# Attention value matmuls gathered behind a step's last key tile, and the softmax sums turned by transposes

## The chip, the core and the metric

The kernel runs on one core of a Trainium2 chip. The metric is the device time of one execution in microseconds (us); the time before is the median of three runs.

## What is computed

Two transformer blocks over 1024 latent positions and 256 context positions, model width 1024. The first has two layers, each with a grouped-query attention beside a convolution, a gated recurrence and a Fourier mix; the second has one latent attention of 16 heads beside a state-space scan, then a feed-forward part. The change touches only the two attentions:

```python
def attend(qb, k, v):                       # first block: 4 query heads, 2 key/value heads, width 64
    s = jnp.einsum("bhgqd,bhkd->bhgqk", qb, k).astype(jnp.float32) * (HEAD_DIM ** -0.5)
    p = jax.nn.softmax(s, axis=-1).astype(v.dtype)
    return jnp.einsum("bhgqk,bhkd->bhgqd", p, v)

def attend_2(q_nope, q_rope, k_nope, k_rope, v):      # second block: 16 heads, value width 64
    s = (jnp.einsum("bqhd,bkhd->bhqk", q_nope, k_nope)
         + jnp.einsum("bqhr,bkr->bhqk", q_rope, k_rope)) * ATTN_SCALE
    p = jax.nn.softmax(s.astype(jnp.float32), axis=-1).astype(v.dtype)
    return jnp.einsum("bhqk,bkhd->bqhd", p, v)
```

Keys are the 1024 latent positions and the 256 of the context: 1280, or ten tiles of 128. The first block's first layer also lets the 256 context queries attend to the two context tiles.

## The kernel before

Both attentions work in **steps**: one head and one block of queries (512, or the 256 of the context). The first block (GQA) has 8 full steps and 4 context steps in its first layer and 8 full steps in its second; the second block's latent attention (MLA) has 32 full steps. That makes 48 full steps of ten key tiles and 4 steps of two.

A step has two parts, and the second part of a step runs beside the first part of the next one. `put_max` finds the largest score of each query, roughly: TensorE multiplies queries by keys (L600 in GQA, L1350 in MLA, twelve matmuls a step), VectorE reduces each result (L459) and all of them (L462), TensorE turns the result into a row (L465), and ScalarE writes that row beside the queries (L466), so that the score matmuls subtract it. `weigh` then loops over the key tiles: scores on TensorE (L613 and L614 in GQA, L1360 to L1362 in MLA) into one of three PSUM tiles `t`, the exponential on ScalarE into a tile `e` (L501), and the running sum of the `e` tiles: two of three on GpSimd (`ea`, L492 then L495), the third on VectorE (`eb`). L519 adds `eb` to `ea` at the end.

The **value matmuls** (L480) multiply a tile of values (128 keys by 64 columns, the stationary operand) with a tile `e` (128 by 512, moving), all in float32. The two matmuls of a pair write the two halves of `o`: the even key tile partitions 0 to 63, the odd one 64 to 127, and each half is summed up by itself. A pair is sent while the loop runs, as soon as one later tile (GQA) or two (MLA) wait behind it:

```python
            waiting.append((v(j), e))
            self.dense(wait)
            if len(waiting) >= lag + 2:
                values([waiting.pop(0), waiting.pop(0)])
```

`weigh_end` finishes a step: four matmuls of `ea` with a column of ones give the 512 sums as four columns (L533), VectorE takes the reciprocal (L535), four transposes spread it (L538), ScalarE copies the upper half of `o` (L540), VectorE adds the halves (L541) and scales them (L542), and the result is stored. It is called inside the next step, behind key tile `tail` (the first number of `GQA_STEPS` and `MLA_STEPS`), so its matmuls stand among the next step's scores. `self.small` is the PSUM tag for its small tiles: `t` in GQA, `mm` (three tiles as well, shared with L1350) in MLA.

The rows of an engine are not in the order of the code: a scheduler that builds the program moves an instruction ahead of others where its operands let it. `dense(us)` asks for that much work of another part of the program (projections, L344 and L213) to be laid between.

Of the kernel before, what the change touches and what calls it, by code (L numbers as in the profile page):

```python
# [16 lines left out]
ALU = mybir.AluOpType  # L17
AX = mybir.AxisListType
# [3 lines left out]
P = 128  # L22
# [55 lines left out]

GQA_STEPS = 4, 4, 1, 0.5
MLA_STEPS = 3, 5, 2, 0.4

FOURIER_WAIT = 1.0
HGRN_WAIT = 12.0, 1.0, 3.0, 2.0, 2.0, 3.0
# [4 lines left out]
class Kern:  # L90
# [377 lines left out]
    def weigh(self, pool, out, keys, n, scores, v, beside, pieces, steps):  # L468

        V, G, S, PE = self.V, self.G, self.S, self.PE
        tail, ahead, lag, wait = steps
        o = self.psum("o")[:, :n]
        waiting, sent = [], []

        def values(pair):
            for h, (vj, e) in enumerate(pair):
                PE.matmul(o[64 * h:64 * h + 64], vj, e, start=not sent, stop=len(sent) == len(keys) // 2 - 1)  # L480
            sent.append(1)


        sums = {}

        def count(i, e):
            E = V if i % 3 == 2 else G
            if E not in sums:
                sums[E] = [e]
            elif len(sums[E]) == 1:  # L490
                total = self.ctmp(pool, "ea" if E is G else "eb", (P, 512), 2)[:, :n]
                E.tensor_tensor(total, sums[E][0], e, op=ALU.add)  # L492
                sums[E] = [total, total]
            else:
                E.tensor_tensor(sums[E][0], sums[E][0], e, op=ALU.add)  # L495

        done = 0
        for i, j in enumerate(keys):
            s = scores(j)
            e = self.ctmp(pool, "e", (P, 512), 6)[:, :n]  # L500
            S.activation(e, s, AF.Exp)  # L501
            count(i, e)
            waiting.append((v(j), e))
            self.dense(wait)
            if len(waiting) >= lag + 2:
                values([waiting.pop(0), waiting.pop(0)])
            if i == tail:
                self.weigh_end()
            while beside and done < pieces and done * (len(keys) - ahead) < (i + 1) * pieces:
                done += 1  # L510
                next(beside, None)
        for _ in beside or ():
            pass
        self.weigh_end()
        while waiting:
            values([waiting.pop(0), waiting.pop(0)])
        total = sums[G][0]
        if V in sums:
            G.tensor_tensor(total, total, sums[V][0], op=ALU.add)  # L519
        self.pending = pool, out, o, total  # L520

    def weigh_end(self):
        if not self.pending:
            return
        pool, out, o, total = self.pending
        self.pending = None
        V, S, PE = self.V, self.S, self.PE

        n = o.shape[1]
        nq = n // P  # L530
        t = self.psum(self.small)
        for a in range(nq):
            PE.matmul(t[:, a:a + 1], total[:, a * P:(a + 1) * P], self.one)  # L533
        r = self.tmp("sl", (P, 4), bufs=3)[:, :nq]
        V.reciprocal(r, t[:, :nq])  # L535
        b = self.psum(self.small)[:, :n]
        for a in range(nq):
            PE.transpose(b[:, a * P:(a + 1) * P], r[:, a:a + 1].to_broadcast([P, P]), self.ident)  # L538
        u = self.tmp("nt")[0:64, :n]
        S.activation(u, o[64:128], AF.Copy)  # L540
        V.tensor_tensor(u, o[0:64], u, op=ALU.add)  # L541
        V.tensor_tensor(u, u, b[0:64], op=ALU.mult)  # L542
        self.store(out, u)
# [42 lines left out]
    def gqa(self, pool, layer, src, need_ctx, y):  # L586
# [22 lines left out]
        def weigh(i, t0, m, h, b, beside, pieces):  # L609
            def scores(j):  # L610
# [7 lines left out]
            self.weigh(pool, y[2 + i][64 * h:64 * h + 64, t0:t0 + m], keys, m, scores,  # L618
                       lambda j: vt[:, j, i], beside, pieces, GQA_STEPS)


        for i in range(2):
            ks[i] = self.gqa_keys(pool, kd, i)
            qs[i] = self.gqa_queries(pool, src[f"q{i}"], layer, n)
            self.dense(4.0)
            last = None
            for t0, m in ALL if n == TA else LAT:
                for h in range(2):
                    b, piece, pieces = maxima(i, t0, m, h)
                    if last:  # L630
                        weigh(*last, piece, pieces)
                    else:
                        for _ in piece:
                            pass
                    last = i, t0, m, h, b
            weigh(*last, None, 0)
# [669 lines left out]
    def mla(self, pool, more, kv, done, beside, y):  # L1306
# [48 lines left out]
        def weigh(p, h, t0, m, beside):  # L1355
            def scores(j):
# [9 lines left out]
            self.weigh(pool, y[p][64 * h:64 * h + 64, t0:t0 + m], range(nk), m, scores, lambda j: v[:, j, a], beside, 12,  # L1366
                       MLA_STEPS)

# [6 lines left out]
        for p in range(8):  # L1375
            for h in range(2):
                for t0, m in LAT:

                    now = maxima(p, h, t0, m)
                    if last:  # L1380
                        weigh(*last, now)
                    else:
                        for _ in now:
                            self.dense(MLA_WAIT[2])
                        self.dense(MLA_WAIT[3])
                    last = p, h, t0, m
                    if p in (1, 7):
                        next(beside, None)
                    if t0 == 0 and p + h == 0:
                        operands(0, 1)  # L1390
                    elif t0 == 0:

                        nxt = 2 * p + h + 1
                        if nxt < 16:
                            operands(nxt // 2, nxt % 2)
                        if nxt in (4, 6, 10):
                            vt[len(vt)] = values(len(vt))
# [659 lines left out]
```

## Time and profile before

| | |
|---|---|
| time, median of 3 runs | 4227.44 us (4225.31 to 4230.69) |
| the profiled execution | 4237.05 us, of it a span of 4234.8 us |
| TensorE busy | 3954.1 us, 93% of the span |
| VectorE, ScalarE, GpSimd busy | 2392.5, 1685.9 and 1518.5 us (56%, 40%, 36%) |
| value matmuls (L480), busy | 238.5 us in MLA, 142.8 us in GQA |
| matmuls of the sums (L533), busy | 32.3 us in MLA, 18.8 us in GQA |
| mean granted TensorE clock | 0.96 of full speed |

Busy time of TensorE is modelled from starts, and neighbouring matmuls overlap in it: what one costs is read from the distance between starts. A float32 matmul leaves two records, two passes, so that a pair of value matmuls is "x4" in a row, a single one "x2". PEld is the loading of the stationary operand.

### The profile page before, as it was taken

The numbers are of one execution on the slowest core, as the hardware profiler recorded it, in microseconds if no ns is written. First come the engines' busy times: TensorE is split into PE (matmuls) and PEld (weight loads), VectorE is DVE, ScalarE is ACT, GpSimd is POOL, SyncE is SP. The second block draws the span as 40 slices with busy tenths as digits, with TensorE's granted clock in tenths as the row PEclk, the third lists the DMA queues.
The fourth block names the chain that finished last, engine by engine and source line by source line (L and its number), as shares of the span: only waits on it lengthen the run. The fifth ranks groups of instructions, "written<-read, shape, count | busy, mean of one in ns | idle before, by whom it ended". The sixth has DMA issues, their size and how long they took to land.

```text
span 4234.8 us, 55709 instructions
## 1 busy us (share of the span) xinstructions
PE 3954.1 (93%) x19762; PEld 2918.6 (69%) x19762; DVE 2392.5 (56%) x4158; ACT 1685.9 (40%) x3047; POOL 1518.5 (36%) x1336
## 2 busy tenths in 40 slices
PE   6999999999999988988999979999999989999998
PEld 3765577667775567666677665655555979988987
DVE  6355487855455487678778774554445365324331
ACT  5333444345334544354343343333334334333332
POOL 3223301126314321154122233455455444445443
PEclk8999999999999989998999999999999989999999
DMA  5541122256541221254534566422212364333232
GB/s 175 165 127 60 53 82 91 85 170 208 170 154 58 63 72 59 88 189 128 164 123 159 184 204 186 127 76 60 48 41 80 120 208 127 95 114 121 93 112 86
DMA packets 273914, 500.26 MB, mean 118 GB/s; under 512 B 30978, under 2 KB 76578, under 8 KB 270628
## 3 DMA queue, kind: packets, MB, share of 16 engines
q1 hardware_dynamic: 269636, 467.75, 35.2%
q0 software_dynamic: 4000, 28.97, 2.9%
q8 instruction: 155, 2.54, 0.3%
q14 instruction: 123, 1.01, 0.1%
HBM read 377.39 MB, written 119.21 MB: 117 GB/s over the span
## 4 chain that ended last, share of the span: by engine, by line
PE 43%; DVE 7%; DMA 3%; issue 2%; ACT 1%; POOL 1%; SPq 0%; DVEq 0%; ACTq 0%; POOLq 0%
PE mm L213 21%; PE o L480 5%; PE mm L344 4%; PE t L1360 2%; PE mm L1350 2%; DVE sp L1165 2%; PE t L1361 2%; PE t L1362 2%; PE t L1589 1%; PE o L1567 1%; PE mm L533 1%; PE t L1524 1%; DMA xt<-xtok 0%; ACT sw L1557 0%; POOL wl L204 0%
## 5 line engine op out<-in xcount | busy, mean ns | idle before, releaser
L204 POOL TENSOR_TENSOR wl<-wr,wh 128x512 fp32r<-128x512 f32 (+2 forms) x641 | 861.0, 1350 | 1555.7 <-ACT wh L203 1346.2
L203 ACT ACTIVATE wh<-wr 128x512 fp32r<-128x512 f32 (+1 forms) x822 | 502.5, 620 | 793.7 <-PE mm L213 246.5
L344 PE MATMUL mm<-xh,wh 128*128 128x512 f32 (+1 forms) x1704 | 667.0, 392 | 11.8 <-DVE sp L169 2.9
L344 PE MATMUL mm<-xh,wl 128*128 128x512 f32 (+1 forms) x1704 | 652.0, 383 | 5.4 <-POOL wl L204 5.3
L344 PE MATMUL mm<-xl,wh 128*128 128x512 f32 (+1 forms) x1704 | 652.9, 384 | 1.8 <-POOL xl L324 1.2
L501 ACT ACTIVATE e<-t 128x512 f32<-128x512 f32 (+1 forms) x488 | 287.4, 594 | 504.7 <-PE t L1362 320.5
L495 POOL TENSOR_TENSOR ea<-ea,e 128x512 f32<-128x512 f32 x240 | 307.3, 1280 | 377.9 <-ACT e L501 365.9
L344 PEld LDWEIGHTS mm<-xh,wh 128*128 128x128 f32 x1704 | 332.1, 195 | 86.3 <-issue 9.5
L344 PEld LDWEIGHTS mm<-xh,wl 128*128 128x128 f32 x1704 | 331.9, 195 | 74.7 <-POOL wl L204 9.5
L344 PEld LDWEIGHTS mm<-xl,wh 128*128 128x128 f32 x1704 | 333.2, 196 | 66.9 <-issue 7.6
L213 PE MATMUL mm<-fxh,wh 128*128 128x512 f32 (+2 forms) x1056 | 339.6, 323 | 2.9 <-ACT fxh L1741 2.1
L213 PE MATMUL mm<-fxh,wl 128*128 128x512 f32 (+2 forms) x1056 | 341.3, 323 | 0.0
L213 PE MATMUL mm<-fxl,wh 128*128 128x512 f32 (+2 forms) x1056 | 340.6, 323 | 0.4 <-DVE fxl L1742 0.3
L459 DVE TENSOR_REDUCE sm<-mm 128x1 f32<-128x512 f32 (+1 forms) x384 | 209.8, 590 | 52.3 <-PE mm L1350 52.1
L480 PE MATMUL o<-e,v 128*64 128x512 f32 x640 | 238.5, 618 | 0.0
L213 PEld LDWEIGHTS mm<-fxh,wh 128*128 128x128 f32 x1056 | 201.4, 191 | 19.0 <-ACT fxh L1741 2.6
L213 PEld LDWEIGHTS mm<-fxl,wh 128*128 128x128 f32 x1056 | 201.9, 191 | 17.4 <-DVE fxl L1742 1.7
L213 PEld LDWEIGHTS mm<-fxh,wl 128*128 128x128 f32 x1056 | 201.9, 191 | 15.5
L204 DVE TENSOR_TENSOR wl<-wr,wh 128x512 fp32r<-128x512 f32 x181 | 134.9, 757 | 72.5 <-ACT wh L203 64.3
L459 DVE TENSOR_REDUCE sm<-t 128x1 f32<-128x512 f32 (+1 forms) x200 | 112.7, 590 | 80.0 <-PE t L600 78.8
L1779 DVE TENSOR_SCALAR fc<-gs,vecs 128x512 f32<-128x512 f32 x44 | 54.5, 1238 | 165.3 <-ACT gs L1775 165.2
L480 PE MATMUL o<-e,vt 128*64 128x512 f32 (+1 forms) x336 | 142.8, 608 | 0.0
(469 smaller groups left out, 8032.9 us busy)
## 6 DMA issues: line engine op xcount, KB each, us to landing
wr<-w_mod SPq DMA_DIRECT2D x192, 256.0 KB, 3.0
wr<-w_in SPq DMA_DIRECT2D x190, 256.0 KB, 3.0
wr<-w_up SPq DMA_DIRECT2D x176, 256.0 KB, 2.6
wr<-w_out SPq DMA_DIRECT2D x144, 256.0 KB, 3.1
wr<-w_down SPq DMA_DIRECT2D x80, 256.0 KB, 2.7
q<-qd POOLq DMA_DIRECT2D x16, 768.0 KB, 6.7
rope<-rope SPq DMA_DIRECT2D x20, 512.0 KB, 4.4
k<-kd POOLq DMA_DIRECT2D x16, 640.0 KB, 7.8
```

The lines of the kernel that those rows point to most:

```text
L203: self.S.activation(hi, raw, AF.Copy)
L204: (next(subs) if subs else self.G).tensor_tensor(lo, raw, f32(hi), op=ALU.subtract)
L213: self.PE.matmul(out, a, b, start=i == 0, stop=i == n - 1)
L344: self.PE.matmul(ps, a, b, start=at + i == 0, stop=at == k_tiles - 1 and i == 2)
L459: V.tensor_reduce(m[:, a, c:c + 1], scores(a, c), axis=AX.X, op=ALU.max, negate=True)
L480: PE.matmul(o[64 * h:64 * h + 64], vj, e, start=not sent, stop=len(sent) == len(keys) // 2 - 1)
L495: E.tensor_tensor(sums[E][0], sums[E][0], e, op=ALU.add)
L501: S.activation(e, s, AF.Exp)
L1165: V.scalar_tensor_tensor(c, u[:, s0 + a:s0 + a + n], cw[:, a:a + 1], c, op0=ALU.mult, op1=ALU.add)
L1350: PE.matmul(s, qt[h][:, 0, t0 + a * P:t0 + (a + 1) * P], kt[h][:, 0, c0:c0 + w])
L1360: PE.matmul(s, kh, qh, start=True, stop=False)
L1361: PE.matmul(s, kh, ql, start=False, stop=False)
```

## The change

The value matmuls leave the loop: `weigh` keeps all `e` tiles of a step and sends the matmuls behind the last key tile, the two halves of `o` by turns. For that there are 13 `e` tiles in place of 6. The `lag` leaves the two tuples. In `weigh_end` the sums come another way: `ea` is turned by four transposes (L527 of the changed kernel, 128x128 each), and VectorE adds up each row of 128 (L529), then takes the reciprocal in place (L531).

```diff
-GQA_STEPS = 4, 4, 1, 0.5
-MLA_STEPS = 3, 5, 2, 0.4
+GQA_STEPS = 4, 4, 0.5
+MLA_STEPS = 3, 5, 0.4
...
-        tail, ahead, lag, wait = steps
+        tail, ahead, wait = steps
         o = self.psum("o")[:, :n]
-        waiting, sent = [], []
-
-        def values(pair):
-            for h, (vj, e) in enumerate(pair):
-                PE.matmul(o[64 * h:64 * h + 64], vj, e, start=not sent, stop=len(sent) == len(keys) // 2 - 1)
-            sent.append(1)
+        es = []
...
             s = scores(j)
-            e = self.ctmp(pool, "e", (P, 512), 6)[:, :n]
+            e = self.ctmp(pool, "e", (P, 512), 13)[:, :n]
             S.activation(e, s, AF.Exp)
             count(i, e)
-            waiting.append((v(j), e))
+            es.append(e)
             self.dense(wait)
-            if len(waiting) >= lag + 2:
-                values([waiting.pop(0), waiting.pop(0)])
...
         self.weigh_end()
-        while waiting:
-            values([waiting.pop(0), waiting.pop(0)])
+        for i, (j, e) in enumerate(zip(keys, es)):
+            h = 64 * (i % 2)
+            PE.matmul(o[h:h + 64], v(j), e, start=i < 2, stop=i >= len(keys) - 2)
...
         for a in range(nq):
-            PE.matmul(t[:, a:a + 1], total[:, a * P:(a + 1) * P], self.one)
+            PE.transpose(t[:, a * P:(a + 1) * P], total[:, a * P:(a + 1) * P], self.ident)
         r = self.tmp("sl", (P, 4), bufs=3)[:, :nq]
-        V.reciprocal(r, t[:, :nq])
+        V.tensor_reduce(r.rearrange("p (a o) -> p a o", o=1), t[:, :n].rearrange("p (a k) -> p a k", k=P), axis=AX.X,
+                        op=ALU.add)
+        V.reciprocal(r, r)
```

Behind the deleted lines the changed kernel's line numbers are four to six smaller: its scores are L1356 to L1358, its maxima L1346, its value matmuls L510, its spreading transposes L534.

What stands in the queues shows how the scheduler took it. The numbers behind names tell tiles apart. First TensorE at the end of a steady MLA step; before:

```order
L1360 MATMUL t_25153<-q1_21819,k1_21821 128x512
L1361 MATMUL t_25153<-q1_21819,k1_21821 128x512
L1362 MATMUL t_25153<-q1_21819,k1_21821 128x512
L480 MATMUL o_25029<-e_25134,v_23721 64x512
L480 MATMUL o_25029<-e_25141,v_23721 64x512
L465 MATMUL mm_25164<-ident_68,sr_25162 1x128 x4
L480 MATMUL o_25029<-e_25150,v_23721 64x512
L480 MATMUL o_25029<-e_25157,v_23721 64x512
L1360 MATMUL t_25176<-q0_21818,k0_21820 128x512
```

and of the changed kernel, the same step:

```order
L510 MATMUL o_25063<-e_25068,v_23746 64x512
L510 MATMUL o_25063<-e_25084,v_23746 64x512
L510 MATMUL o_25063<-e_25098,v_23746 64x512
L510 MATMUL o_25063<-e_25113,v_23746 64x512
L510 MATMUL o_25063<-e_25144,v_23746 64x512
L465 MATMUL mm_25191<-ident_68,sr_25189 1x128 x4
L510 MATMUL o_25063<-e_25157,v_23746 64x512
L510 MATMUL o_25063<-e_25165,v_23746 64x512
L510 MATMUL o_25063<-e_25172,v_23746 64x512
L510 MATMUL o_25063<-e_25179,v_23746 64x512
L510 MATMUL o_25063<-e_25186,v_23746 64x512
L1356 MATMUL t_25211<-q0_21838,k0_21840 128x512
```

The ten value matmuls of this step stood in seven runs before (1, 1, 1, 1, 2, 2, 2), and stand in two runs of five now, parted by the transposes of L465.

Next TensorE in the middle of the same step, where the sums of the step before it are taken; before:

```order
L480 MATMUL o_25029<-e_25050,v_23721 64x512
L533 MATMUL mm_25084<-one_72,ea_24908 128x1 x4
L1360 MATMUL t_25107<-q1_21819,k1_21821 128x512
L1361 MATMUL t_25107<-q1_21819,k1_21821 128x512
L1362 MATMUL t_25107<-q1_21819,k1_21821 128x512
L1360 MATMUL t_25120<-q1_21819,k1_21821 128x512
L1361 MATMUL t_25120<-q1_21819,k1_21821 128x512
L538 MATMUL mm_25091<-ident_68,sl_25089 128x128 x4
```

and in the changed kernel:

```order
L527 MATMUL mm_25116<-ident_68,ea_24941 128x128 x4
L1356 MATMUL t_25153<-q1_21839,k1_21841 128x512
L1357 MATMUL t_25153<-q1_21839,k1_21841 128x512
L1358 MATMUL t_25153<-q1_21839,k1_21841 128x512
L1356 MATMUL t_25161<-q1_21839,k1_21841 128x512
L1357 MATMUL t_25161<-q1_21839,k1_21841 128x512
L1358 MATMUL t_25161<-q1_21839,k1_21841 128x512
L1356 MATMUL t_25168<-q1_21839,k1_21841 128x512
L1357 MATMUL t_25168<-q1_21839,k1_21841 128x512
L1358 MATMUL t_25168<-q1_21839,k1_21841 128x512
L1356 MATMUL t_25175<-q1_21839,k1_21841 128x512
L534 MATMUL mm_25124<-ident_68,sl_25121 128x128 x4
```

Between the turning of the sums and the spreading of their reciprocals five score matmuls stood before, ten stand now.

Last VectorE at that place; before:

```order
L459 TENSOR_REDUCE sm_25036<-mm_25072 128x1
L535 RECIPROCAL sl_25089<-mm_25084 128x4
L542 TENSOR_TENSOR nt_25096<-nt_25096,mm_25091 64x512
L459 TENSOR_REDUCE sm_25036<-mm_25101 128x1
L459 TENSOR_REDUCE sm_25036<-mm_25104 128x1
```

and in the changed kernel (`e_25157` is the exponential of the step's sixth key tile):

```order
L459 TENSOR_REDUCE sm_25070<-mm_25106 128x1
L529 TENSOR_REDUCE sl_25121<-mm_25116 128x4
L487 TENSOR_TENSOR eb_25159<-e_25098,e_25157 128x512
L531 RECIPROCAL sl_25121<-sl_25121 128x4
L538 TENSOR_TENSOR nt_25129<-nt_25129,mm_25124 64x512
L459 TENSOR_REDUCE sm_25070<-mm_25134 128x1
```

The reduction is new, and an addition of `e` tiles now stands between it and the reciprocal.

## Rows read from the trace of the kernel before

**Rows 1.** Busy time by stage: stretch, length, each engine's busy us, TensorE clock, DMA
```profile
240.00:480.00 240.00, 230.45 (x963) 134.81 (x961) 126.08 (x238) 93.61 (x157) 83.27 (x74) 0.96 0.21 66
1240.00:1480.00 240.00, 236.41 (x988) 136.33 (x986) 127.14 (x229) 105.69 (x169) 88.47 (x76) 1.00 0.23 71
2700.00:3160.00 460.00, 458.01 (x1894) 250.52 (x1894) 227.90 (x432) 174.42 (x296) 225.66 (x190) 1.00 0.28 68
```

**Rows 2.** What TensorE waited for from 2700 to 3160 us: total us, times, longest
```profile
PE t L266 <- DVE rsy L236: 2.0, 1, 2.0
```

**Rows 3.** Busy time of one steady MLA step, columns as in rows 1
```profile
2864.69:2884.09 19.40, 19.40 (x80) 10.26 (x78) 9.30 (x18) 7.16 (x12) 9.48 (x9) 1.00 0.35 73
```

**Rows 4.** TensorE in order of time in that step: start us, duration us
```profile
2863.69 1.08 PE L480 MATMUL o<-e,v 128*64 128x512 f32 x4
...
2870.52 1.07 PE L480 MATMUL o<-e,v 128*64 128x512 f32 x2
2871.52 0.50 PE L1360 MATMUL t<-q,k 128*128 128x512 f32 x1
...
2872.56 0.95 PE L533 MATMUL mm<-one,ea 128*128 128x1 f32 x8
2873.36 0.48 PE L1361 MATMUL t<-q,k 128*128 128x512 f32 x1
...
2873.91 0.60 PE L538 MATMUL mm<-ident,sl 128*128 128x128 f32 x4
2874.27 0.60 PE L1350 MATMUL mm<-k,q 128*128 128x256 f32 x2
...
2878.38 0.39 PE L1361 MATMUL t<-q,k 128*128 128x512 f32 x1
2878.61 0.40 PE L1362 MATMUL t<-q,k 128*128 128x512 f32 x1
2878.94 1.08 PE L480 MATMUL o<-e,v 128*64 128x512 f32 x4
2879.95 0.51 PE L1360 MATMUL t<-q,k 128*128 128x512 f32 x1
2880.29 0.40 PE L1361 MATMUL t<-q,k 128*128 128x512 f32 x1
...
2883.08 1.08 PE L480 MATMUL o<-e,v 128*64 128x512 f32 x4
```

**Rows 5.** TensorE at the end of the last MLA step, in order of time
```profile
3244.72 1.94 PE L480 MATMUL o<-e,v 128*64 128x512 f32 x8
3248.23 1.05 PE L533 MATMUL mm<-one,ea 128*128 128x1 f32 x8 [1.57 <-POOL ea L519]
```

**Rows 6.** Loading of the stationary operands in the run of rows 5
```profile
3245.20 0.57 PEld L480 LDWEIGHTS o<-e,v 128*64 128x64 f32 x4 [0.29 <-issue]
```

**Rows 7.** TensorE, VectorE and ScalarE in order of time in that steady step
```profile
2865.27 0.40 PE L1362 MATMUL t<-q,k 128*128 128x512 f32 x1
...
2865.76 0.60 ACT L501 ACTIVATE e<-t 128x512 f32<-128x512 f32 x1 [0.33 <-PE t L1362]
...
2866.08 3.82 DVE L459 TENSOR_REDUCE sm<-mm 128x1 f32<-128x512 f32 x7
...
2878.41 1.24 ACT L501 ACTIVATE e<-t 128x512 f32<-128x512 f32 x2 [3.63 <-PE t L1362]
```

**Rows 8.** Groups of VectorE: the reductions and first additions; busy us, mean ns
```profile
L459 DVE TENSOR_REDUCE sm<-mm 128x1 f32<-128x512 f32 (+1 forms) x384 | 209.8, 590 | 52.3 <-PE mm L1350 52.1
...
L492 DVE TENSOR_TENSOR eb<-e 128x512 f32<-128x512 f32 x22 | 15.1, 686 | 2.2 <-ACT e L501 2.2
```

**Rows 9.** VectorE's reciprocal of the sums: ns least, median, most
```profile
L535 DVE RECIPROCAL sl<-mm x32: 181/183/184, 2620.0 to 3249.3; 128x4 f32<-128x4 f32 x32
```

**Rows 10.** A long wait of TensorE in GQA, and the stretch behind it
```profile
399.26 0.59 PE L286 MATMUL mm<-wl,act 128*4 128x512 f32 x1 [3.56 <-DVE wl L204]
...
398.10:408.30 10.20, 8.53 (x23) 5.09 (x24) 8.56 (x12) 7.01 (x10) 3.74 (x3) 0.50 0.38 119
```

## The prediction

> **What bounds the kernel now.** I read the busy time by stage first, because the page's share of 93% for TensorE is a mean over stages that differ. In GQA and MLA TensorE is busy nearly throughout: 230.45 of 240 us and 236.41 of 240 us around the two GQAs, and 458.01 of 460 us in the steady part of MLA, at the full clock there [rows 1]. The view of waits then tells whether those busy stretches hide any waiting: over the 460 us TensorE waited once, for 2.0 us [rows 2]. One steady step lasts 2883.08 - 2863.69 = 19.39 us from value run to value run [rows 4], and in it TensorE is never idle, while VectorE works 9.30 us, GpSimd 9.48 us and ScalarE 7.16 us [rows 3]. So in this stage a microsecond less on TensorE is a microsecond less in the span, until another engine is late. The question is therefore what the new order costs on TensorE, and whether VectorE, which gets more work, stays ahead.
>
> **Value matmuls: the price of a run.** In order of time ordinary matmuls of 512 columns start 0.23 us apart (2878.38 to 2878.61). From the L1362 at 2878.61 to the L1361 at 2880.29 there are 1.68 us, with a pair of value matmuls and one L1360 between. Two ordinary distances are 0.46, so this pair costs 1.22 us [rows 4]. A value matmul that stands alone keeps TensorE from 2870.52 to 2871.52, 1.00 us, as long as the pair does (2878.94 to 2879.95, 1.01) [rows 4]: its other half of the array stays empty. What a further pair in the same run costs shows only at the end of the last step, where two pairs stand together: 1.94 us against 1.08 for one, so 0.86 more [rows 4, 5]. Hence a run costs 0.36 us for itself, on entering and leaving, and 0.86 us for each slot, and a slot takes a pair or a single. A run of five with its halves by turns is three slots.
>
> I counted runs and slots over the whole order of both builds. MLA: 221 runs with 222 slots become 67 runs with 188 slots. That is 221 x 0.36 + 222 x 0.86 = 270.5 us against 67 x 0.36 + 188 x 0.86 = 185.8 us: 84.7 us less. In a steady step it is 7 x 1.22 = 8.54 against 2 x (1.22 + 2 x 0.86) = 5.88, so 2.66 us. The full steps of GQA: 119 runs and 119 slots become 93 and 120, since there the scheduler still sends six value matmuls singly among the maxima, as fillers: 26 x 0.36 - 0.86 = 8.5 us less. The context steps lose one run of half width, which I leave out.
>
> **A rule against it.** In the run of two pairs four loads of stationary operands take 0.57 us and lie within the 1.94 us [rows 5, 6], so the 0.86 already holds them. The Trainium skill, "TensorE: Matmul & The Clock Gate", part 3 (the mechanism), says that a weight load overlaps running matmuls only where their row groups differ. All value matmuls use the same 128 rows, so by that sentence the loads of each further pair would come on top. The row speaks against it, and the sum goes by the row; but it is a single run, so this stays a rival.
>
> **The sums.** Four matmuls with a column of ones hold TensorE from 2872.56 to 2873.36, 0.80 us. Four transposes of the same 128x128 form, L538, hold it from 2873.91 to 2874.27, 0.36 us [rows 4]. The new L527 has that form, so 0.44 us less in each of 48 full steps: 21 us. Nothing is the other bound, if turning a dense tile costs as much as the matmuls did.
>
> **VectorE.** It adds a reduction of 128x512 from PSUM, 0.59 us by L459 [rows 8], in each full step; the reciprocal remains, 0.18 us [rows 9]. That makes 9.9 us a step against a new step of 19.39 - 2.66 - 0.44, about 16.3 us, so VectorE does not become the bound by its sum. But there is a wait: the reciprocal now stands behind an addition (L487) that needs the exponential of the sixth key tile, and TensorE's L534 needs the reciprocal. From the start of that tile's last score matmul, ScalarE begins 0.49 us later and takes 0.60 (2865.27, 2865.76) [rows 7], the addition 0.69 [rows 8], the reciprocal 0.18: about 2.0 us. TensorE has that matmul and seven more before L534, 8 x 0.23 = 1.84 us. So it waits about 0.2 us a step, and the next scores, the last four maxima and the values stand behind it: 32 x 0.2 = 6 us. The bounds are nothing, and some 1.0 us a step (reduction, reciprocal and their handovers with nothing before them), 32 us. In GQA the turned sums hold one of the three tiles `t`, which scores and maxima need too, for up to 0.59 us longer in 20 steps: between nothing and 12 us, and I take 3, since other matmuls stand in between.
>
> **What the scattered values covered.** A step's scores now follow each other with nothing but maxima between: 30 x 0.23 + 8 x 0.23 + 4 x 0.12 + 2 x 0.36, about 10 us (0.12 for the maxima of 256 columns, half the distance). ScalarE needs ten exponentials at 0.62 (two in 1.24) [rows 7], 6.2 us, and the copy of `o`; three score matmuls, 0.69 us, still take longer than one exponential. VectorE's reductions begin 2866.08 - 2863.69 = 2.39 us after a value run of 1.01 starts [rows 4, 7], 1.4 us into a step, and run back to back, seven in 3.82 us. With 9.9 us of work in all VectorE is through at about 11.3 us. TensorE needs its result (L465) only behind the first five value matmuls, at 10 + 2.9 = 12.9 us. So the cover of 1.6 us holds, and I price this at nothing. Were VectorE later than that, each microsecond a step costs 32 us. GpSimd's last additions have the whole value phase and three key tiles of the next step, and the 13 `e` tiles let ScalarE run ahead into the next step. The transfers of the next head stay where they were, behind the last score that reads the old ones; a step of 16 us in place of 19 is still well above their landing.
>
> **The sum.** -84.7 - 8.5 - 21 + 6 + 3 = -105 us against the profiled execution's 4237.05 us: 4132 us. The median of the runs shown is 0.23% lower, 4227.44 us, so the forecast for the median is 4122 us. A change within 0.2%, 8 us, I count as none; it is about what such a measurement can tell.
>
> **Rivals.**
> A. VectorE or the PSUM tiles become late within a step: TensorE waits 1 to 2 us more in each MLA step, at L534, at the last maxima or at L465. For it speaks that VectorE has only those 1.6 us in hand; against it, its 9.9 us in a step of 16. It gives back 32 to 64 us: 4154 to 4186 us.
> B. Loads are not hidden in long runs. 188 - 67 = 121 further pairs in MLA at 0.57 us [rows 6] give back 69 us: 4191 us. The skill's sentence above says this; the one run in rows 5 shows the opposite.
> C. Slower. New waits of TensorE in each step let its clock fall. In GQA a wait of 3.56 us for weights stands beside a stretch of 10.2 us at the lower level, 1.2 of 2.4 GHz, 0.50 granted [rows 10]. Such a stretch costs half its length, 5.1 us, so from 105 / 5.1 = 21 of them the gain is gone. With one in each of 32 MLA steps the time is 4122 + 163 = 4285 us. Against it: waits of a few tenths are far from 3.56 us, and the steady part of MLA held 1.00 with its 2.0 us wait [rows 1, 2].
> D. The change does not do what it says: the freed time returns as waits for transfers or in the projections that are laid between, and the time stays at 4220 to 4235 us. Against it, the DMA share is 0.28 in MLA [rows 1], and little but attention is left there.
>
> **How the numbers follow.** The sum with small waits has 0.73. Its own range is 4094 to 4150: the sum with no new wait is 4113, and the scheduler may have closed GQA's gaps by some 20 us, which I can't price; above, the 32 us of the reduction's bound. A has 0.14, B 0.04, C 0.05, D 0.04. The range of 8 in 10 takes in A up to about its middle: 4094 to 4172. Faster by over 0.2% are the sum, A and B, 0.91; D is the same, 0.04; C is slower, 0.05.
>
> **What would show it.** The steady MLA step falls from 19.39 to about 16.5 us. Its ten value matmuls take two runs of about 2.73 us from start to next start, not seven of 1.0. L527 takes about 0.36 us. TensorE's waits in MLA name the reciprocal L531, briefly, and L465 does not wait. GQA gets shorter by no more than some 15 us in all. A run of five longer than 3 us means B; waits of over 1 us a step before maxima or L465 mean A; a clock under 1.00 between the first and last MLA step means C. If GQA grows instead, the fillers or the longer use of `t` were mispriced.

## The result, and the profile after

The changed kernel takes 4120.3 us (median of 4 runs, 4114.03 to 4122.74), the kernel before 4226.7 us (median of 4, 4225.31 to 4230.69). The ratio is 0.9744, with a 95% interval from 0.9728 to 0.9761. The forecast was 4122 us. That the total came out to 2 us is partly luck, as the stages show: MLA gained 8 us less than forecast and GQA 10 us more.

The page of the changed kernel, its span and each engine's busy time:

```profile
span 4119.5 us, 55376 instructions
PE 3827.2 (93%) x19562; PEld 2892.6 (70%) x19562; DVE 2426.4 (59%) x4210; ACT 1683.2 (41%) x3047; POOL 1536.1 (37%) x1336
```

TensorE lost 127 us of busy time and its share stayed at 93%: a share says nothing about a change that shortens the work and the span together. Busy time by stage, columns as in [rows 1]; the last row is one steady MLA step:

```profile
240.00:480.00 240.00, 230.02 (x955) 133.16 (x954) 133.95 (x255) 96.99 (x168) 91.82 (x79) 0.95 0.20 60
1240.00:1480.00 240.00, 229.09 (x977) 134.63 (x976) 141.47 (x243) 124.34 (x193) 102.75 (x88) 0.97 0.23 70
2620.00:3060.00 440.00, 431.31 (x1983) 269.90 (x1982) 274.15 (x514) 189.16 (x322) 254.85 (x206) 1.00 0.33 83
2848.72:2865.49 16.77, 16.50 (x75) 9.99 (x74) 10.10 (x19) 7.17 (x12) 9.99 (x10) 1.00 0.14 35
```

In these 440 us of MLA the clock is at 1.00, and VectorE has 10.10 us of work in a step of 16.77. TensorE, 99.6% busy in [rows 1], is now 98.0% busy: there is a wait that was not there before. The view of waits names it, for TensorE from 2620 to 3060 us (total us, times, longest):

```profile
PE mm L534 <- DVE sl L531: 6.0, 20, 0.5
PE mm L1346 <- DVE nt L538: 2.7, 4, 1.3
```

The first of these 440 us are no steady steps yet, since projections are laid between: all four waits of L1346 fall before 2730 us, and from there to 3060 us the view names L534 alone, 19 times, 5.5 us. That is 0.29 us a step of idle time; what the wait costs is read below from start to start. One steady step on TensorE, in order of time, answers to [rows 4]:

```profile
2848.72 2.79 PE L510 MATMUL o<-e,v 128*64 128x512 f32 x10
2851.45 0.50 PE L1356 MATMUL t<-q,k 128*128 128x512 f32 x1
...
2856.62 0.60 PE L527 MATMUL mm<-ident,ea 128*128 128x128 f32 x4
2856.98 0.47 PE L1356 MATMUL t<-q,k 128*128 128x512 f32 x1
...
2857.53 0.40 PE L1358 MATMUL t<-q,k 128*128 128x512 f32 x1
...
2859.15 0.40 PE L1356 MATMUL t<-q,k 128*128 128x512 f32 x1
2859.82 0.65 PE L534 MATMUL mm<-ident,sl 128*128 128x128 f32 x4 [0.28 <-DVE sl L531]
2860.23 0.60 PE L1346 MATMUL mm<-k,q 128*128 128x256 f32 x2
...
2862.24 2.79 PE L510 MATMUL o<-e,v 128*64 128x512 f32 x10
2864.97 0.60 PE L465 MATMUL mm<-ident,sr 128*1 128x128 f32 x4
2865.49 2.79 PE L510 MATMUL o<-e,v 128*64 128x512 f32 x10
```

A run of five value matmuls takes 2851.45 - 2848.72 = 2.73 us to the next start, as forecast. The turning L527 takes 0.36. From the last score matmul ahead of L534 to L534 there are 0.67 us, where an ordinary distance is 0.23: the wait costs 0.44 us, of which only 0.28 is recorded as idle, since the matmul ahead is modelled as busy until 2859.55. The transposes themselves hold TensorE for 0.41 us (2859.82 to 2860.23), not 0.36. So this place costs 0.49 us more than it would without the wait, in the mean of 20 steady steps 0.50. (x10 is a run of five.) VectorE, ScalarE and GpSimd at that place:

```profile
2857.26 0.69 DVE L529 TENSOR_REDUCE sl<-mm 128x4 f32<-128x512 f32 x1
2858.66 1.02 DVE L487 TENSOR_TENSOR eb<-e 128x512 f32<-128x512 f32 x1 [0.70 <-ACT e L496]
2859.60 0.17 DVE L531 RECIPROCAL sl<-sl 128x4 f32<-128x4 f32 x1
```

```profile
2857.96 0.60 ACT L496 ACTIVATE e<-t 128x512 f32<-128x512 f32 x1 [0.48 <-DVE sl L529]
```

```profile
2856.47 2.66 POOL L490 TENSOR_TENSOR ea<-ea,e 128x512 f32<-128x512 f32 x2 [0.80 <-ACT e L496]
```

The sums are added up by 2857.95. The reciprocal starts 1.65 us later, because L487 stands ahead of it and waits for the sixth exponential of the step, which ScalarE begins at 2857.96 and ends at 2858.56. This is the wait that the forecast named, but it is longer: the addition takes 1.02 us, not 0.69. GpSimd has an addition under way until 2859.13. In each of 20 steady steps of gather_only the same addition starts as one of GpSimd's ends and takes 0.69 or 0.70 us; here it takes 1.02 in 19 of 20. That GpSimd's addition holds it up fits these rows; no experiment took it away.

For the comparison of kernels I cut each profiled span at four places that all of them have: the first matmul of the maxima of each GQA layer, the start of the last copy of `o` of each attention, and the last matmul of the scan ahead of MLA. "Step" is the median distance of the copies of `o` over 24 steady MLA steps.

| kernel | GQA, both layers | MLA | step | all the rest |
|---|---|---|---|---|
| before | 425.4 | 724.5 | 19.36 | 3085.0 |
| after | 402.9 | 640.1 | 16.78 | 3076.5 |
| gather_only | 401.8 | 642.2 | 16.92 | 3071.2 |
| sums_only | 423.4 | 707.6 | 18.82 | 3073.6 |
| bufs_only | 424.7 | 724.2 | 19.36 | 3077.8 |
| gqa_lag_2 | 412.9 | 727.2 | 19.36 | 3085.4 |
| even_runs | 406.2 | 622.8 | 15.97 | 3080.8 |
| halves_apart | 407.2 | 701.4 | 18.53 | 3065.6 |
| even_ones | 402.5 | 622.8 | 16.09 | 3070.6 |
| even_tail_2 | 404.9 | 609.4 | 15.47 | 3072.3 |
| tail_2 | 402.6 | 629.5 | 16.31 | 3065.3 |
| even_ones_tail_2 | 402.8 | 619.8 | 15.91 | 3065.3 |

Each kernel was measured beside the kernel before, which took 4224.7 to 4230.3 us in these measurements, so kernels of different measurements are compared by their ratios to it. No experiment edits the rest, and yet it differs by up to 20 us between profiles. Differences of total time below some 10 us are therefore not read as the edit's, and the stages decide. From before to after, MLA gives 84.4 us and GQA 22.5; the other 8.5 us of the profiled difference of 115.3 us are not the attentions'.

### The profile page after: what moved, and what is told of

Same layout as the page of the kernel before. It is cut to its first block, busy times and chain, and to the rows that moved or that the text cites. A ratio compares the mean times of both kernels' runs of the same rounds, so it can differ in the third digit from the quotient of the medians.

```text
span 4119.5 us, 55376 instructions
## 1 busy us (share of the span) xinstructions
PE 3827.2 (93%) x19562; PEld 2892.6 (70%) x19562; DVE 2426.4 (59%) x4210; ACT 1683.2 (41%) x3047; POOL 1536.1 (37%) x1336
## 3 DMA queue, kind: packets, MB, share of 16 engines
q14 instruction: 123, 1.01, 0.1%
## 4 chain that ended last, share of the span: by engine, by line
PE 37%; DVE 11%; DMA 4%; ACT 2%; issue 2%; POOL 1%; SPq 0%; DVEq 0%; ACTq 0%; POOLq 0%
PE mm L213 22%; PE mm L344 5%; PE o L510 4%; DVE sm L459 3%; DVE sp L1161 2%; PE mm L1346 1%; DVE eb L487 1%; PE o L1563 1%; PE t L1585 1%; PE t L1357 1%; PE t L1358 1%; PE t L1520 1%; PE t L1356 1%; ACT sw L1553 1%; DMA xt<-xtok 0%
## 5 line engine op out<-in xcount | busy, mean ns | idle before, releaser
L490 POOL TENSOR_TENSOR ea<-ea,e 128x512 f32<-128x512 f32 x240 | 325.5, 1356 | 170.1 <-ACT e L496 161.8
L459 DVE TENSOR_REDUCE sm<-mm 128x1 f32<-128x512 f32 (+1 forms) x384 | 207.6, 589 | 17.3 <-PE mm L1346 16.7
L510 PE MATMUL o<-e,v 128*64 128x512 f32 x640 | 175.8, 602 | 0.0
L487 POOL TENSOR_TENSOR ea<-e 128x512 f32<-128x512 f32 (+1 forms) x52 | 65.8, 1265 | 237.0 <-ACT e L496 204.5
L459 DVE TENSOR_REDUCE sm<-t 128x1 f32<-128x512 f32 (+1 forms) x200 | 112.3, 589 | 55.3 <-PE t L596 53.8
```

The lines of the kernel that those rows point to most:

```text
L459: V.tensor_reduce(m[:, a, c:c + 1], scores(a, c), axis=AX.X, op=ALU.max, negate=True)
L510: PE.matmul(o[h:h + 64], v(j), e, start=i < 2, stop=i >= len(keys) - 2)
```

## Experiments

### gather_only and sums_only: one part of the change each

gather_only is the changed kernel with the sums as before, as the diff shows; sums_only is the kernel before with the last two hunks of the change, its new sums.

```diff
-            PE.transpose(t[:, a * P:(a + 1) * P], total[:, a * P:(a + 1) * P], self.ident)
+            PE.matmul(t[:, a:a + 1], total[:, a * P:(a + 1) * P], self.one)
...
-        V.tensor_reduce(r.rearrange("p (a o) -> p a o", o=1), t[:, :n].rearrange("p (a k) -> p a k", k=P), axis=AX.X,
-                        op=ALU.add)
-        V.reciprocal(r, r)
+        V.reciprocal(r, t[:, :nq])
```

> Value matmuls gathered as in the change, sums by matmuls with a column of ones as before. Mine (the gain is the gathered values; the turned sums save 0.44 us a full step and give 0.3 us a step back in MLA as the wait at L534): MLA has 63 runs and 188 slots, the same slots as the change, so about 4120 + 21 - 10 = 4131 us. Rival 1 (the turned sums carry much of the gain): above 4160 us. Rival 2 (the turned sums cost more than they save): 4110 us or less.

> Value matmuls as before (223 runs in MLA), sums turned by transposes and added up on VectorE. Mine: 48 x 0.44 = 21 us less than before, less a few us of waits: 4206 to 4212 us. Rival (the sums' turning is free on TensorE but waits eat it): 4227 us. Rival (it carries much of the gain): under 4180 us.

gather_only took 4121.18 us (ratio 0.9744, 0.9727 to 0.9761), which is the whole gain of the change; I had expected 10 us less of it. sums_only took 4209.06 us (ratio 0.9954, 0.9938 to 0.9969), as expected: alone, the turned sums are worth 21 us, 16.9 of them in MLA (0.54 a step) and 2.0 in GQA, with no wait of TensorE in the view from 2700 to 3160 us. So the two parts don't add up: beside gathered values the turned sums bring 642.2 - 640.1 = 2.1 us in MLA, where alone they bring 16.9. In gather_only TensorE waits far less from 2620 to 3060 us, and not for a reciprocal:

```profile
PE mm L465 <- DVE sr L462: 0.8, 1, 0.8
PE mm L1344 <- DVE nt L536: 0.5, 1, 0.5
PE mm L1344 <- DVE sm L459: 0.2, 1, 0.2
```

### bufs_only: the kernel before with 13 `e` tiles

```diff
-            e = self.ctmp(pool, "e", (P, 512), 6)[:, :n]
+            e = self.ctmp(pool, "e", (P, 512), 13)[:, :n]
```

> The kernel before with 13 e tiles in place of 6, nothing else; the order of TensorE keeps 221 runs. Mine: no change, 4227 us, within 5 us. Rival (ScalarE waiting for a free e tile was part of what the change removed, above all in GQA, where the gain was larger than forecast): 10 us or more below, 4217 us or less.

It took 4230.03 us (ratio 1.0001, 0.9992 to 1.001), with the same step to 0.01 us. The longer ring of tiles alone is worth nothing.

### even_runs: runs of six and four in place of five and five

```diff
+        def values(lo, hi):
+            for i, (j, e) in list(enumerate(zip(keys, es)))[lo:hi]:
+                h = 64 * (i % 2)
+                PE.matmul(o[h:h + 64], v(j), e, start=i < 2, stop=i >= len(keys) - 2)
+
+        values(0, 6)
         for _ in beside or ():
             pass
         self.weigh_end()
-        for i, (j, e) in enumerate(zip(keys, es)):
-            h = 64 * (i % 2)
-            PE.matmul(o[h:h + 64], v(j), e, start=i < 2, stop=i >= len(keys) - 2)
+        values(6, len(keys))
```

> The change with the ten value matmuls sent as six, then the rest of the maxima, then four: in steady MLA steps runs of 6 and 4 in place of 5 and 5, so 5 slots and not 6; over MLA 165 slots in 71 runs against 188 in 67. GQA stays at 120 slots. Mine (a run costs by slots of a pair, 0.86 us each): 23 x 0.86 less, 4 runs x 0.3 more: about 19 us below the change, 4101 us; the steady step 0.86 us shorter. Rival (a run costs by its number of matmuls): 4120 us, no change against the change.

It took 4111.4 us (ratio 0.9722, 0.9705 to 0.9739). MLA fell by 17.3 us and the step by 0.81, one slot of 0.86 less: this term is right. GQA grew by 3.3 us and the rest of the profile by 4.3, so that the total fell by 9 us, not 19. TensorE in a steady step:

```profile
2864.84 2.80 PE L508 MATMUL o<-e,v 128*64 128x512 f32 x12
2867.57 0.60 PE L465 MATMUL mm<-ident,sr 128*1 128x128 f32 x4
2868.09 1.94 PE L508 MATMUL o<-e,v 128*64 128x512 f32 x8
2869.96 0.50 PE L1360 MATMUL t<-q,k 128*128 128x512 f32 x1
```

Six matmuls take 2.73 us, no longer than five in the changed kernel, and four take 1.87.

### halves_apart: the same matmuls, first all of the lower half, then all of the upper

```diff
-        for i, (j, e) in enumerate(zip(keys, es)):
+        for i, (j, e) in sorted(enumerate(zip(keys, es)), key=lambda x: x[0] % 2):
```

> The change with a step's value matmuls sent all even tiles first, then all odd ones: the same number of matmuls in about as many runs of MLA (67), but neighbours mostly write the same half of o; steady steps stand as runs of 3 and 7. Mine (a half works beside the other only where the two stand next to each other): 3 slots, then 2 + 5 - 1 = 6, 9 in place of 6, so 3 x 0.86 = 2.6 us a steady step and about 80 us more in all: near 4200 us. Rival 1 (each half keeps its own queue, so the order inside a run is of no matter): the run of 7 takes 5 slots, 8 in place of 6, about 45 us more: near 4165 us. Rival 2 (what counts is how seldom TensorE goes in and out of such runs): 4120 us, no change.

It took 4180.16 us (ratio 0.9899, 0.9877 to 0.9921): 60 of the 106 us (65 by the ratios) are lost by the order of the halves alone. Rival 2 is out. TensorE in a steady step:

```profile
2867.88 2.79 PE L510 MATMUL o<-e,v 128*64 128x512 f32 x6
2870.60 0.60 PE L465 MATMUL mm<-ident,sr 128*1 128x128 f32 x4
2871.12 4.52 PE L510 MATMUL o<-e,v 128*64 128x512 f32 x14
2875.57 0.50 PE L1356 MATMUL t<-q,k 128*128 128x512 f32 x1
```

The first run holds three matmuls of one half and takes 2.72 us, three slots: nothing overlaps. The second holds two of the lower half and then five of the upper, and takes 4.45 us, five slots (runs of one to five slots measured 1.00, 1.87, 2.72, 3.58 and 4.44 us over these kernels). My theory, that only the neighbours at the change of half overlap, gave six. Here two overlap, and the step has the eight slots of rival 1. But a queue of its own for each half, rival 1, fails elsewhere: a run of ten, five and five, takes 7.07 us, eight slots where that rival has five. What fits the runs of six, seven, eight and ten (4.44, 4.45, 5.35, 7.07 us; five, five, six and eight slots) is that one matmul can wait for its half while the next, of the other half, starts. That was read from the result and not tested further.

### gqa_lag_2: pairs of GQA sent one key tile later

The kernel before with the lag of MLA in GQA too.

```diff
-GQA_STEPS = 4, 4, 1, 0.5
+GQA_STEPS = 4, 4, 2, 0.5
```

> The kernel before, with GQA's pairs sent one key tile later (lag 2 as in MLA), nothing else. In GQA its 42 pairs take 1.25 us from start to next start in the mean, in MLA 1.01. Mine (GQA gained more than forecast because its pairs stood waiting for the exponential of their second tile, and any later sending removes this): the mean falls to about 1.0, and 42 x 0.24 = 10 us go: 4217 to 4222 us by the before of these runs near 4230. Rival (the extra gain of GQA is the larger runs or the lane work laid in): 4230 us, no change.

It took 4215.22 us (ratio 0.9977, 0.9967 to 0.9988), 9.5 us below the kernel before of the same measurement, as expected. GQA fell by 12.5 us. What went is a wait that the view of waits doesn't show. In the kernel before, TensorE and ScalarE at the end of a GQA step:

```profile
1322.48 1.45 PE L480 MATMUL o<-e,vt 128*64 128x512 f32 x4
1323.87 0.50 PE L613 MATMUL t<-qa,ka 128*128 128x512 f32 x1
```

```profile
1322.21 0.60 ACT L501 ACTIVATE e<-t 128x512 f32<-128x512 f32 x1 [1.19 <-PE t L614]
```

The pair takes 1.39 us to the next start, not 1.01: its second matmul needs the exponential that ends at 1322.81, 0.33 us after the pair began. The first one runs meanwhile, so no idle time is recorded. Over the 42 pairs that stood by themselves the mean was 1.25 us, 42 x 0.24 = 10 us. In gqa_lag_2 the 36 that stand by themselves take 1.01 each, and the same place reads:

```profile
1315.02 1.08 PE L480 MATMUL o<-e,vt 128*64 128x512 f32 x4
1316.03 0.50 PE L613 MATMUL t<-qa,ka 128*128 128x512 f32 x1
```

### even_ones and even_tail_2: the sums in even_runs, by ones or two key tiles earlier

even_ones is even_runs with the sums of before; even_tail_2 is even_runs with `MLA_STEPS = 2, 5, 0.4`, which takes the turned sums behind key tile 2 and no longer 3 (the second diff; the first is even_ones).

```diff
-            PE.transpose(t[:, a * P:(a + 1) * P], total[:, a * P:(a + 1) * P], self.ident)
+            PE.matmul(t[:, a:a + 1], total[:, a * P:(a + 1) * P], self.one)
```

```diff
-MLA_STEPS = 3, 5, 0.4
+MLA_STEPS = 2, 5, 0.4
```

> The version with six and four value matmuls, with the sums by matmuls with a column of ones as before the change. Mine (in the gathered order the turned sums save 0.5 us a step and lose 0.3 in waiting): steady step 0.1 to 0.2 us longer than even_runs' 15.97, total within 5 us of its 4111 us. Rival (the turned sums are worth their 0.44 us a step once runs are even): 15 us or more above even_runs, 4126 us.

> The version with six and four value matmuls, and in MLA the end of the last step called behind the third key tile, not the fourth: the reciprocal then stands ahead of the addition that needs the sixth exponential. Mine (the wait of 0.3 us a step at the spreading transposes is what eats the turned sums' saving): steady step 15.97 - 0.3 = 15.7 us, 8 to 10 us below even_runs' 4111: 4102 us. Rival (the reduction on VectorE delays the maxima, wherever it stands): no change, 4111 us.

even_ones took 4098.04 us (ratio 0.9701, 0.9684 to 0.9718), 13 us below even_runs, 9 by the ratios; I had expected the same within 5. By stages the two are alike in MLA (622.8 us both, a step 0.12 longer), differ by 3.7 in GQA and by 10.2 in the rest, which neither edits, so this pair says only that the turned sums win next to nothing behind key tile 3. even_tail_2 took 4081.92 us (ratio 0.9665, 0.9646 to 0.9684), the fastest kernel of the study. I had expected 4102 and a step of 15.7. MLA fell by 13.4 us against even_runs and the step by 0.50, to 15.47: that is what the place of L538 costs in even_runs from start to start, and not the 0.3 that I had taken. In the order of that step, on VectorE,

```profile
2872.21 0.68 DVE L533 TENSOR_REDUCE sl<-mm 128x4 f32<-128x512 f32 x1
2872.92 0.18 DVE L535 RECIPROCAL sl<-sl 128x4 f32<-128x4 f32 x1
2874.26 0.68 DVE L542 TENSOR_TENSOR nt<-nt,mm 64x512 f32<-64x512 f32 x1 [1.16 <-PE mm L538]
```

the reciprocal follows the reduction at once, since no addition stands between, and TensorE's whole list of waits from 2620 to 3060 us is

```profile
PE mm L213 <- DVE sm L459: 0.5, 1, 0.5
PE mm L1350 <- DVE nt L542: 0.5, 1, 0.5
```

### tail_2 and even_ones_tail_2: is it the wait, or the earlier place?

tail_2 is the changed kernel with the number alone, even_ones_tail_2 is even_ones with it.

```diff
-MLA_STEPS = 3, 5, 0.4
+MLA_STEPS = 2, 5, 0.4
```

> The changed kernel with one number changed: the sums of a step are turned and spread behind key tile 2 of the next step instead of key tile 3; the order gives the same 188 slots of value matmuls in MLA, in runs of three and seven. My theory: the turned sums gave nothing beside the gathered values because the reciprocal stood behind an addition that waits for an exponential; two key tiles earlier that addition stands behind it, the wait of about 0.3 us a step at the spreading transposes is gone and with it the shorter waits of the maxima. The steady MLA step falls from 16.78 to about 16.35 us, the MLA stage from 640 to about 626 us, the time from 4120 to about 4107 us. Rival 1, the turned sums are themselves no cheaper for TensorE than the ones matmuls: the step stays at 16.7 to 16.8, the time at 4115 to 4125. Rival 2, moving the sums earlier makes them wait for GpSimd's last addition: a wait in front of the turning transposes, the step longer than 16.8, the time over 4125.

> Values in even runs of six and four, sums by the matmuls with a column of ones, and these placed behind key tile 2. With the ones nothing waited behind key tile 3, so by my theory there is nothing to win: the step stays at 16.1 us (16.09 behind tile 3), the MLA stage at 622 to 624, the time within 6 us of 4098. Against the same kernel with turned sums (step 15.47, stage 609) the turning is then worth about 0.6 us a step and some 14 to 20 us in all, once its wait is gone. Rival, the earlier place itself wins, whatever makes the sums: the step falls to about 15.5 to 15.7 and the stage to about 610, and the turning is worth nothing in any place.

tail_2 took 4100.47 us (ratio 0.9701, 0.9688 to 0.9714), with a step of 16.31 and a stage of 629.5 us. The list of waits has no L534 and 0.5 us of L1346 where it had 6.0 and 2.7. even_ones_tail_2 took 4095.28 us (ratio 0.9693, 0.9677 to 0.9709). Its step fell too, from 16.09 to 15.91, which neither theory had. The rows of even_ones show why: behind the spreading transposes it has a wait of its own, in no list of TensorE's waits.

```profile
2880.09 0.39 PE L1360 MATMUL t<-q,k 128*128 128x512 f32 x1
2880.38 0.50 PE L1348 MATMUL mm<-k,q 128*128 128x512 f32 x1
2880.71 0.39 PE L1358 MATMUL t<-q,k 128*128 128x512 f32 x1
```

The distances are 0.29 and 0.33 us where ordinary ones are 0.23: 0.16 a step, the same in gather_only. The profile puts the loading of this maximum's stationary operand down to L540 (L542 of the kernel before), which reads the spread sums in an `mm` tile. In even_ones_tail_2 both distances are 0.23, as they are behind key tile 3 in the kernels with turned sums. So the 0.47 that tail_2 wins go with the 0.50 of the place of L534, and the 0.18 here are nearly all another wait. What is left between the two kinds of sums behind key tile 2, where no steady step waits, is the turning's: even_tail_2 has a step of 15.47, 0.44 less, the forecast's price to the digit, and 10.4 us less in MLA. Where the 0.44 comes from stands in the rows of TensorE, first by ones, then turned:

```profile
2866.77 0.95 PE L531 MATMUL mm<-one,ea 128*128 128x1 f32 x8
2867.58 0.49 PE L1359 MATMUL t<-q,k 128*128 128x512 f32 x1
```

```profile
2871.56 0.60 PE L531 MATMUL mm<-ident,ea 128*128 128x128 f32 x4
2871.92 0.48 PE L1361 MATMUL t<-q,k 128*128 128x512 f32 x1
```

They take 0.81 us and 0.36 us from start to next start.

## Why the prediction was right, and where it was not

**The bound.** That TensorE's time is the span's time in MLA held: over the whole study MLA moved with TensorE's rows.

**Value matmuls in MLA: right.** Forecast 84.7 us less, measured alone 82.3 (gather_only). The slot of 0.86 us was right in runs of every length. A removed run was worth a little less than 0.36: the step fell by 2.44 us, not 2.66, and with one slot of 0.86 less this leaves 1.58 for five runs, 0.32 each.

**Rival B: wrong.** In the run at 2862.24 the loads lie inside the 0.43 us from one pass to the next:

```profile
2862.73 0.14 PEld L510 LDWEIGHTS o<-e,v 128*64 128x64 f32 x2 [0.29 <-issue]
2863.16 0.14 PEld L510 LDWEIGHTS o<-e,v 128*64 128x64 f32 x2 [0.28 <-issue]
```

and the run of five lasts 2.73 us, where loads on top would have made it 3 us and more. The sentence of the Trainium skill ("TensorE: Matmul & The Clock Gate", part 3, the mechanism) that a load overlaps running matmuls only where the row groups differ is not what these rows show: all ten use the same 128 rows.

**The sums: the step that failed.** "0.44 us less in each of 48 full steps: 21 us" was right as a price in MLA: 0.54 a step alone, 0.44 where nothing waited. The step that failed is the wait: "So it waits about 0.2 us a step" was right in its place and cause, but the place costs 0.50, more than the turning saves. The chain from the start of the last score matmul of the sixth tile (2857.53) to L534 (2859.82) takes 2.29 us, not "about 2.0", against 1.85 of TensorE's eight matmuls. The excess is the addition, 0.94 from its start to the reciprocal's where the sum had 0.69 (beside GpSimd's, above), and two handovers of 0.10 and 0.05 that it had at nothing. The transposes behind it take 0.05 longer too, which no term held.

That the step still gained 16.92 - 16.78 = 0.14 comes from the wait of 0.16 at a maximum that gather_only has and the changed kernel has not: 0.45 saved, 0.50 lost, 0.16 not waited for, with some hundredths left. In all, the sums were to bring 12 us; they brought 2.1 in MLA, and in GQA the stages with turned sums are 1.1 to 3.7 us longer in the three pairs with gathered values, which was not looked into.

The place of the reciprocal in VectorE's queue, not the cost of the turning, decided it in MLA, as the pairs of kernels show: behind key tile 3 the turning is worth 0.12 and 0.14 us a step (even_ones against even_runs, gather_only against after), behind key tile 2 0.44.

**VectorE.** Its reduction takes 0.69 us in MLA:

```profile
L529 DVE TENSOR_REDUCE sl<-mm 128x4 f32<-128x512 f32 x32 | 22.1, 691 | 8.7 <-PE mm L527 8.7
```

The 0.59 of [rows 8] was misread. It is a mean over two widths ("+1 forms"): of those L459 the 256 with 512 columns take 0.68 us and the 128 with 256 columns 0.41. VectorE did not become the bound, and in the list of waits above L465 does not stand: the cover held. Rival A is out as such, at 0.50 us a step in place of 1 to 2. C is out too: the clock is 1.00 from 2620 to 3060 us, and over the whole MLA stage 0.99, where the kernel before has 0.98.

**GQA: right sign, a term missing.** Forecast 8.5 us for the runs, "no more than some 15 us in all"; the stages fell by 22.5. Of this gqa_lag_2 got 12.5 without gathering anything, by taking away the wait inside the pairs. I had read 1.22 us for a pair off MLA, where both exponentials are done in time, and used it in GQA, where they are not; the view of waits shows nothing there, and only the distance of starts does. I had said that the scheduler may close gaps in GQA worth 20 us "which I can't price"; the distances in the trace of before would have priced half of them.

So the sum of 105 us met 106 because two errors offset each other. For MLA it has 84.7 + 14.1 - 6 = 92.8 us and the stage gave 84.4; for GQA it has 8.5 + 7.0 - 3 = 12.5, and the stages gave 22.5.

## What to carry to other kernels

Float32 matmuls that fill half the array, as here, are worth gathering by turns of the halves and in even numbers: what counts is the number of slots and, with a third of a microsecond each, of runs. When the work of one engine is made cheaper by handing part of it to a second one, look first at what stands ahead of it in the second engine's queue, and move the place before judging the price. And read a pair's cost in its own stage, from start to next start, since a wait inside a pair is in no list of waits, and a listed wait can cost more than its idle time (0.50 us where 0.28 was listed).

## What the runs showed of the hardware that was not expected

- A lone matmul of 64 columns costs as much as a pair (1.00 and 1.01 us), and a run of five as much as one of six (2.73 us both).
- The order of issue matters between halves: by turns, ten matmuls take five or six slots; sorted by half, eight (3 + 5 in a steady step), and the time rises by 60 us.
- A second matmul of a pair can wait for its operand for up to 0.8 us (pairs in GQA from 1.01 to 1.82 us) while the record shows TensorE busy. So can a maximum behind the spreading transposes, for 0.16 us a step.
- Turning a dense 128x512 tile (four transposes, 0.36 us) is cheaper than four float32 matmuls with one column (0.81 us); the rows show eight records for the latter and four for the former.
- VectorE's addition of two 128x512 tiles took about 1.0 us where it ran beside an addition on GpSimd, and 0.69 where it did not (changed kernel and gather_only, steady steps).
